# Two hybrid transformer blocks on one core: a written order of loads and smaller steps in the second block's attention stage

## The chip, the cores and the metric

The kernel runs on one core of a Trainium2 chip. The core has a matrix engine (TensorE, PE in the profile; its weight loads are PEld), a vector engine (VectorE, DVE), a scalar engine (ScalarE, ACT), GpSimd (POOL) and SyncE (SP). Each engine executes its own instructions in the order in which they stand in its stream, and waits on semaphores. DMAs are issued from SP, ACT or POOL and carried out by 16 DMA engines. The metric is the time of one execution in microseconds (us).

## The reference, cut to what matters

`x` has 512 tokens of 1024 channels, in float32. A first block (four mixers and a feed-forward network) is followed by a second one. The change touches only the first half of the second block:

```
h = rms(x, norm1) * (1 + sc1) + sh1
u, q, k, v = split(h @ w_in)             # 512 | 512 | 128 | 128 columns
# S5: a diagonal complex scan over the tokens, 32 groups of 16 channels, 64 states each
y = C_re s_re - C_im s_im + d_skip * u   # s = scan(a, B u)
z = gelu(y)
y_ssm = z * sigmoid(z @ w_glu + b_glu)
# attention: 8 query heads, 2 key/value heads, window of 128 tokens, one sink per head
q, k = rms(q per head), rms(k per head)
y_attn = softmax(q k / 8 + relative bias, with sink) v
x = x + g1 * (concat(rms(y_ssm), rms(y_attn)) @ w_out)
```

A modulated, gated feed-forward network with a convolution of width 3 follows and is unchanged.

## The kernel before

Activations lie transposed, channels on the 128 partitions and 512 tokens along the row. Every large product is done three times with numbers split into a high and a low part (`whi`, `wlo` for weights, `hl` for activations). A weight piece comes in with one SP DMA into a `raw` buffer (two of them), ACT copies its high part, and DVE subtracts the low part; for `w_glu` and `w_out` (w6, w7) ACT writes minus the high part and a POOL DMA adds the weights to it. There are five pairs of `whi`/`wlo`. A piece is loaded when the piece ahead of it is first used.

The stage of the second block is a list of steps, ORDER, of which PE's instructions are issued in exactly this order (`manual_schedule` with PE alone). What the other engines, SP included, do is ordered by a planner at build time: it takes an instruction when its data are ready by the planner's own estimate of times, and of those that are ready the one that stands earlier in the program. On the chip each engine then runs this fixed order, whatever the real times are.

The steps: `U` finishes the product for `u` and sends it through DRAM (`d_u`) to the layout of the scan (`ua`). `kp`, `qp` project keys and values, or queries, for two token tiles, copy the result out of PSUM (`tok`, and `v`) and norm it per head (`head_norm`: DVE, with two small ACT functions between); `kt`, `qt` transpose it. For each quarter q of the S5 channels, `a` is the product with `et`, copied to `z`; `b` rotates `z` by the tables `co`, `si` and runs eight scans on DVE; `c` rotates back into `sp`; `d` makes the outputs `ys` with the tables `tt`, `gt` and sends them through DRAM (`d_z`, eight small stores a quarter), reads them back as `yt` and adds the skip term. `e` is the gelu and the split for `g`, the gated unit. `s`, `t`, `v` are scores and softmax, transposes, and the product with the values, for one head group and token tile. `R`, `p`, `A` are the norms and the output product.

The copies out of PSUM run on ACT or DVE as a letter of EN says (`a`, `v`). The tables `et`, `co`, `si` of all four quarters and `tt`, `gt` of the first two are issued on SP before the list of steps; `tt`, `gt` of the others in step c2; the relative bias `relb` in the first score step of a head group. Buffers that matter: `tab` (six) for `et`, `tt`, `relb` and the probabilities, `tabg` (two) for `gt`, `sp` (two), PSUM `acc` (three), `sc` and `tr` (two each).

Of the kernel before, what the change touches and what calls it, by code (L numbers as in the profile page):

```python
# [17 lines left out]
P = 128  # L18
# [19 lines left out]
NPOS2 = 2  # L38
B2 = 1
TAIL = 4  # L40
ZQ = "assssaaa"
HP = ""
EG = 0
EN = "avaaavaaaaaaaaaaaaavvvvvvvavavvaaaavaaaaaaaaaaaavaavvvvavvvvaaaavvvvaavvvaaaaavavaaavaavvavvvvvvvvvvavvaavvvvvavvaaavaaaavaaavvaaaaaaavvvvvvvaaaaaaaaavvvavvaavaaaav"
EN_AT = {'k1': (0, 4), 'v1': (4, 4), 'q1': (8, 12), 'h1': (20, 8), 'w1': (28, 8), 's1': (36, 8), 'o1': (44, 16), 't1': (60, 46), 'u2': (106, 4), 'z2': (110, 4), 'y2': (114, 4), 'k2': (118, 2), 'v2': (120, 2), 'q2': (122, 4), 'h2': (126, 12), 's2': (138, 12), 't2': (150, 14)}
ORDER = "U kp0 kp1 a0 a1 kt0 b0 qp0 c0 a2 b1 qp1 kt1 b2 c1 d0 a3 c2 qt0 qt1 b3 c3 d1 s0 qp2 s1 s2 t0 d2 t1 d3 e0 s3 e1 qt2 t2 s4 qp3 v0 t3 s5 v1 g0 qt3 g1 g2 t4 g3 s6 v2 v3 s7 t5 R p0 p1 v4 p2 t6 v5 p3 p4 v6 t7 p5 v7 p6 p7 A"
NW = 16
NHL = 5
SUM_E = "vector"
# [183 lines left out]
def build(tc, I, out, PV, PVN, CS, CSN, CS1, CSN1):  # L233
# [1162 lines left out]
    def wt(nm):  # L1396
        return bp.tile([P, S], F32, tag="w", bufs=NW2, name=nm)

    def tab(nm):
        return bp.tile([P, 1024], F32, tag="tab", bufs=6, name=nm)  # L1400

    zT, zhl = [], []
    zs, z2s, cs, ss, sps, ets, tts, gts = {}, {}, {}, {}, {}, {}, {}, {}

    def s5_load(qs):
        for q in qs:
            ets[q] = tab("et")
            nc.sync.dma_start(ets[q], d_et[q])
            cs[q], ss[q] = wt("co"), wt("si")
            nc.sync.dma_start(cs[q], d_rot[q][:, 0])  # L1410
            nc.sync.dma_start(ss[q], d_rot[q][:, 1])

    def s5_load2(qs):
        for q in qs:
            tts[q] = tab("tt")
            nc.sync.dma_start(tts[q], d_t[q].rearrange("p g x -> p (g x)"))
            gts[q] = bp.tile([P, 8, 9 * 16], F32, tag="tabg", bufs=2, name="gt")
            nc.sync.dma_start(gts[q].rearrange("p g x -> p (g x)"), d_g[q])

    s5_load((0, 1))  # L1420
    s5_load2((0, 1))
    s5_load((2, 3))

    def u_out(q, ps):
        t = wt("uT").rearrange("p (s c) -> p s c", s=8)
# [52 lines left out]
            V.tensor_tensor_scan(z2[:, c], mag8[:, q * 8 + g:q * 8 + g + 1].to_broadcast([P, 64]), z[:, c], 0.0, ALU.mult, ALU.add)  # L1478

    def s5_c(q):  # L1480
        if q == 2:
            s5_load2((2, 3))
        z, z2 = zs[q], z2s[q]
        crossed(z, z2, ss[q], -1.0)
        zc = wt("zc")
        (G if "c" in ZC else V).tensor_tensor(zc, z2, cs[q], op=ALU.mult)
        sp = bp.tile([P, 8, 65], F32, tag="sp", bufs=2, name="sp")
        sps[q] = sp
        V.memset(sp[:, :, 0:1], 0.0)
        V.tensor_tensor(sp[:, :, 1:65], z.rearrange("p (g c) -> p g c", g=8),  # L1490
                        zc.rearrange("p (g c) -> p g c", g=8), op=ALU.add)

    def s5_d(q):
        ut = wt("ut")
# [9 lines left out]
            E.dma_start(d_z[q].rearrange("g h t c -> t h g c")[t], ys[16 * t:16 * t + 16])  # L1504
        yt = xp.tile([P, S], F32, tag="x", name="yt")
        nc.gpsimd.dma_start(yt, d_z[q].rearrange("g h t c -> (g h) (t c)"))
        V.scalar_tensor_tensor(yt, ut, V1("ssm_d", q), yt, op0=ALU.mult, op1=ALU.add)
        zT.append(yt)

    def s5_e(n):  # L1510
        if EG and n == 0:
            return
        for q in (range(4) if EG else (2 * n, 2 * n + 1)):
            ge = act(zT[q], zT[q], AF.Gelu_apprx_tanh)
            zz = hl()
            split(zz, zT[q])
            zhl.append(zz)
        tables(ge)
# [16 lines left out]
    def q_p(n):  # L1535
        j, m = n // 2, n % 2
        ps = acc()
        for u in range(2):
            proj_t(ps, wkv[1 + j], h, 2 * m + u, 256, 256 * u)
        qt, qn = wt("tok"), wt("tokn")  # L1540
        copy("q2", n, qt, ps)
        head_norm(bp, wt, [qn.rearrange("p (h a d) -> p h a d", h=8, a=1)], qt, 8)
        tokn["q", n] = qn.rearrange("p (u b x) -> p u b x", u=2, b=2)

# [13 lines left out]


    mixed = [hl() for _ in range(8)]  # L1560
    relbs, probs, pvs = {}, {}, {}
    tot_s, tot_a, r_s, r_a = (wt(n) for n in ("tot_s", "tot_a", "r_s", "r_a"))

    def keep(k, src, cs, tot, first, gain, n, scale=1.0):
# [14 lines left out]
    def swa_s(n):  # L1579

        kv, i, j0, W = window(n)
        if i == 0:
            relbs[kv] = tab("relb").rearrange("p (h y) -> p h y", h=4)
            nc.sync.dma_start(relbs[kv].rearrange("p h y -> p (h y)"), I["relb"][:, kv * 1024:(kv + 1) * 1024])
            V.tensor_scalar(relbs[kv], relbs[kv], -1.0, None, op0=ALU.mult)
        ml = bp.tile([P, 4], F32, tag="ml", bufs=2, name="ml")
        sl = bp.tile([P, 4], F32, tag="sl", bufs=2, name="sl")
        se = bp.tile([P, 4], F32, tag="se", bufs=2, name="se")
# [69 lines left out]
    def ssm_out(k):  # L1658
# [5 lines left out]
        V.scalar_tensor_tensor(t, ps, gm[:, k:k + 1], r_s, op0=ALU.mult, op1=ALU.mult)  # L1664
        G.tensor_tensor(x[k], x[k], t, op=ALU.add)

    steps = dict(U=u_last, a=s5_a, b=s5_b, c=s5_c, d=s5_d, e=s5_e, kp=kv_p, kt=kv_t, qp=q_p, qt=q_t,
                 s=swa_s, t=swa_t, v=swa_v, g=glu, R=norm_s, p=ssm_out, A=norm_a)
    with tc.manual_schedule(engines={mybir.EngineType.PE}):
        for step in ORDER.split():  # L1670
            name = step.rstrip("0123456789")
            with tc.high_priority() if name in HP.split(",") else nullcontext():
                steps[name](*([int(step[len(name):])] if step != name else []))
# [93 lines left out]
```

## Time and profile before

| what | value |
|---|---|
| median of 3 runs | 1274.1 us (1273.36 to 1276.45) |
| the profiled execution, its own time | 1273.53 us |
| its span in the trace | 1271.8 us |
| PE busy | 1220.6 us, 96% of the span |
| PEld busy | 986.8 us, 78% |
| DVE busy | 888.4 us, 70% |
| ACT busy | 512.6 us, 40% |
| POOL busy | 251.8 us, 20% |
| mean granted PE clock | 0.984 |

The page divides the span into 40 slices of about 32 us each and gives each engine's share in tenths. A "chain" is followed back from the last instruction. An arrow as in `PE <- DVE v` means that PE stood idle until the DVE instruction that writes `v` was done.

### The profile page before, as it was taken

How to read it: one execution, taken by the hardware profiler on the slowest of the kernel's cores; microseconds unless marked ns; L12 is line 12 of the kernel's file. 1: busy time of each engine (PE TensorE's matmuls, PEld its weight loads, DVE VectorE, ACT ScalarE, POOL GpSimd, SP SyncE). 2: the span in 40 equal slices, each digit the busy share in tenths (PEclk: the TensorE clock that was granted, in tenths of full speed). 3: DMA queues.
4: the chain of work that ended last, by engine and by line, in shares of the span. 5: the costliest groups of instructions: out<-in, count | busy, mean ns of one | idle time of the engine just before them, and what ended most of it. 6: DMA issues, size and time to landing. Idle time of an engine off the chain costs nothing.

```text
span 1271.8 us, 17124 instructions
## 1 busy us (share of the span) xinstructions
PE 1220.6 (96%) x6269; PEld 986.8 (78%) x6269; DVE 888.4 (70%) x1666; ACT 512.6 (40%) x874; POOL 251.8 (20%) x355
## 2 busy tenths in 40 slices
PE   7899999999999999999999978879999999999998
PEld 6788756567887888878889877758888888888887
DVE  7667858768877967777567578766887655555552
ACT  6334466453333332232324334764643423233330
POOL 1000003103408375573402232022000000000000
PEclk9999999999999999999999986989999999999999
DMA  6531111115466665656546873464364433323321
GB/s 222 150 124 51 51 33 50 51 42 167 131 182 180 214 211 191 200 171 211 171 149 235 241 190 96 111 169 101 92 186 120 123 93 99 99 83 99 100 83 66
DMA packets 165395, 169.87 MB, mean 134 GB/s; under 512 B 12352, under 2 KB 127952, under 8 KB 165312
## 3 DMA queue, kind: packets, MB, share of 16 engines
q1 hardware_dynamic: 154528, 146.96, 38.1%
q0 software_dynamic: 5696, 17.54, 5.4%
q10 hardware_dynamic: 5088, 4.29, 1.0%
q8 instruction: 49, 0.80, 0.3%
q14 instruction: 34, 0.28, 0.1%
HBM read 155.15 MB, written 15.43 MB: 134 GB/s over the span
## 4 chain that ended last, share of the span: by engine, by line
PE 81%; DVE 8%; issue 3%; ACT 3%; DMA 3%; POOL 1%; SPq 0%; POOLq 0%; ACTq 0%; DVEq 0%
PE acc L261 53%; PE sc L261 13%; PE tr L261 10%; PE po L261 2%; DMA raw<-in_w_dram 2%; DVE wlo L381 1%; PE tr L886 1%; ACT whi L374 1%; PE tr L1616 1%; DVE z L1478 1%; DVE z L1467 1%; DVE z L1466 1%; POOL keep L929 0%; DMA ua<-d_u 0%; DVE keep L930 0%
## 5 line engine op out<-in xcount | busy, mean ns | idle before, releaser
L261 PE MATMUL acc<-hl,whi 128*128 128x512 f32 (+1 forms) x1624 | 482.5, 380 | 9.5 <-ACT whi L374 6.1
L374 ACT ACTIVATE whi<-raw 128x1024 fp32r<-128x1024 f32 (+2 forms) x188 | 194.3, 1035 | 409.9 <-PE acc L261 230.6
L261 PEld LDWEIGHTS acc<-hl,whi 128*128 128x128 f32 x1624 | 294.4, 188 | 76.3 <-issue 8.8
L261 PE MATMUL acc<-hl,wlo 128*128 128x512 f32 (+1 forms) x812 | 307.6, 379 | 0.0
L381 DVE TENSOR_TENSOR wlo<-raw,whi 128x1024 fp32r<-128x1024 f32 (+2 forms) x178 | 226.1, 1272 | 110.2 <-ACT whi L374 106.0
L261 PEld LDWEIGHTS acc<-hl,wlo 128*128 128x128 f32 x812 | 152.7, 188 | 30.8 <-issue 2.4
L261 PE MATMUL acc<-hd,whi 128*128 128x512 f32 (+1 forms) x472 | 143.1, 386 | 2.1 <-DVE x L1348 2.1
L261 PE MATMUL acc<-whi,hl 128*128 128x256 f32 (+1 forms) x544 | 111.9, 297 | 6.6 <-DVE v L250 3.3
L261 PEld LDWEIGHTS acc<-hd,whi 128*128 128x128 f32 x472 | 86.9, 188 | 21.7 <-issue 3.1
L261 PEld LDWEIGHTS acc<-whi,hl 128*128 128x128 f32 x544 | 91.4, 200 | 12.0 <-DVE v L250 3.5
L261 PE MATMUL acc<-hd,wlo 128*128 128x512 f32 (+1 forms) x236 | 90.9, 385 | 0.0
L261 PE MATMUL acc<-wlo,hl 128*128 128x256 f32 (+1 forms) x272 | 80.2, 295 | 0.7 <-DVE wlo L381 0.7
L1082 DVE CUSTOM_DVE_ANT_0 wm<-wm,cb 128x512 f32<-128x512 f32 x96 | 75.5, 820 | 5.7 <-DMA wm<-in_wmod_dram 5.6
L261 PE MATMUL tr<-hl,whi 128*128 128x512 f32 (+1 forms) x240 | 72.8, 386 | 0.0
L261 PE MATMUL sc<-hl,whi 128*128 128x512 f32 x208 | 64.9, 393 | 0.0
L261 PEld LDWEIGHTS acc<-wlo,hl 128*128 128x128 f32 x272 | 54.6, 201 | 2.5 <-DVE wlo L381 1.0
L261 PEld LDWEIGHTS tr<-hl,whi 128*128 128x128 f32 x240 | 44.5, 188 | 9.8
L261 PEld LDWEIGHTS acc<-hd,wlo 128*128 128x128 f32 x236 | 44.3, 188 | 9.5
L929 POOL TENSOR_SCALAR_AFFINE_SELECT keep<-keep 128x128 f32<-128x128 f32 x16 | 9.3, 595 | 187.1 <-ACT keep L923 186.3
L261 PE MATMUL tr<-hl,wlo 128*128 128x512 f32 (+1 forms) x120 | 46.3, 386 | 0.0
L261 PEld LDWEIGHTS sc<-hl,whi 128*128 128x128 f32 x208 | 39.1, 188 | 9.0
L1348 DVE TENSOR_TENSOR x<-x,acc 128x512 f32<-128x512 f32 (+1 forms) x49 | 31.6, 655 | 19.2 <-PE acc L261 19.2
(427 smaller groups left out, 1893.5 us busy)
## 6 DMA issues: line engine op xcount, KB each, us to landing
raw<-in_w_dram SPq DMA_DIRECT2D x176, 512.0 KB, 4.3
wm<-in_wmod_dram SPq DMA_DIRECT2D x96, 256.0 KB, 4.0
wlo<-in_w_dram POOLq DMA_DIRECT2D x10, 512.0 KB, 7.9
xk<-in_xT_dram SPq DMA_DIRECT2D x16, 256.0 KB, 4.7
raw<-in_w_dram SPq DMA_DIRECT2D x10, 256.0 KB, 3.2
d_g<-s5g POOLq DMA_DIRECT2D x4, 576.0 KB, 4.6
gt<-d_g SPq DMA_DIRECT2D x4, 576.0 KB, 6.6
w1c<-in_w1k_dram SPq DMA_DIRECT2D x8, 256.0 KB, 5.8
```

The lines of the kernel that those rows point to most:

```text
L261: nc.tensor.matmul(o, lhsT=l, rhs=r, start=start, stop=stop, **k)
L374: act(v(hi)[:, a:b], v(raw)[:, a:b], AF.Copy)
L381: V.tensor_tensor(v(lo)[:, a:b], v(raw)[:, a:b], v(hi.bitcast(F32))[:, a:b], op=ALU.subtract)
L886: nc.tensor.transpose(tp[:, q * P:(q + 1) * P], pr[hh][:, j * P:(j + 1) * P], ident)
L929: G.affine_select(g[:, d], g[:, d], fill=1.0, **past)
L1082: V.tensor_tensor_reduce(wm, wm, cb[:, n * 512:(n + 1) * 512], 1.0, 0.0, ALU.mult, ALU.add, mh[:, n, j:j + 1])
L1348: done[0] = V.tensor_tensor(x[k][:, cs], x[k][:, cs], ps[:, cs], op=ALU.add)
L1466: V.scalar_tensor_tensor(dst[re], src[im], sign, t[im], op0=ALU.mult, op1=ALU.mult)
L1467: V.scalar_tensor_tensor(dst[im], src[re], -sign, t[re], op0=ALU.mult, op1=ALU.mult)
L1478: V.tensor_tensor_scan(z2[:, c], mag8[:, q * 8 + g:q * 8 + g + 1].to_broadcast([P, 64]), z[:, c], 0.0, ALU.mult, ALU.add)
L1616: nc.tensor.transpose(tp[:, m * P:(m + 1) * P], probs[n][:, hh, (j - j0) * P:(j - j0 + 1) * P], ident)
```

## The change

- Query norms become steps of their own (`qn`), and adding the skip term too (`y`, chained so that the quarters come in order). `kt1` stands ahead of `qp1`.
- The loads become steps: `L` (et, co, si of one quarter), `M` (tt, gt of one quarter), `B` (relb and its negation), and `W`, which loads the next weight piece. The loads of SP are issued in the order of the list, as PE's are.
- All four gelus run in `e1`, the last quarter first, the others queued behind it on ACT; `e0` is gone.
- Four copies go from DVE to ACT: `z` of quarters 1 and 2, `ys` of quarter 2, `v` of the second pair of token tiles (in EN: z2 `avva` to `aaaa`, y2 `aava` to `aaaa`, v2 `av` to `aa`).
- Of the eight `d_z` stores of a quarter four were on SP and four on ACT; now four are on POOL and four on ACT.

```diff
--- before.py
+++ after.py
@@ -38,12 +38,12 @@
 NPOS2 = 2
 B2 = 1
 TAIL = 4
-ZQ = "assssaaa"
+ZQ = "aggggaaa"
 HP = ""
 EG = 0
-EN = "avaaavaaaaaaaaaaaaavvvvvvvavavvaaaavaaaaaaaaaaaavaavvvvavvvvaaaavvvvaavvvaaaaavavaaavaavvavvvvvvvvvvavvaavvvvvavvaaavaaaavaaavvaaaaaaavvvvvvvaaaaaaaaavvvavvaavaaaav"
+EN = "avaaavaaaaaaaaaaaaavvvvvvvavavvaaaavaaaaaaaaaaaavaavvvvavvvvaaaavvvvaavvvaaaaavavaaavaavvavvvvvvvvvvavvaavvvvvaaaaaaaaaaaaaaavvaaaaaaavvvvvvvaaaaaaaaavvvavvaavaaaav"
 EN_AT = {'k1': (0, 4), 'v1': (4, 4), 'q1': (8, 12), 'h1': (20, 8), 'w1': (28, 8), 's1': (36, 8), 'o1': (44, 16), 't1': (60, 46), 'u2': (106, 4), 'z2': (110, 4), 'y2': (114, 4), 'k2': (118, 2), 'v2': (120, 2), 'q2': (122, 4), 'h2': (126, 12), 's2': (138, 12), 't2': (150, 14)}
-ORDER = "U kp0 kp1 a0 a1 kt0 b0 qp0 c0 a2 b1 qp1 kt1 b2 c1 d0 a3 c2 qt0 qt1 b3 c3 d1 s0 qp2 s1 s2 t0 d2 t1 d3 e0 s3 e1 qt2 t2 s4 qp3 v0 t3 s5 v1 g0 qt3 g1 g2 t4 g3 s6 v2 v3 s7 t5 R p0 p1 v4 p2 t6 v5 p3 p4 v6 t7 p5 v7 p6 p7 A"
+ORDER = "U L0 kp0 L1 kp1 M0 a0 a1 kt0 b0 qp0 L2 b1 M1 c0 a2 W qn0 c1 kt1 W qp1 L3 d0 B0 b2 a3 W M2 c2 qn1 b3 c3 qt0 qt1 d1 M3 y0 s0 qp2 s1 s2 t0 y1 d2 t1 d3 s3 qn2 y2 y3 e1 qt2 t2 B1 s4 qp3 qn3 v0 t3 s5 v1 g0 qt3 g1 g2 t4 g3 s6 v2 v3 s7 t5 R p0 p1 v4 p2 t6 v5 p3 p4 v6 t7 p5 v7 p6 p7 A"
 NW = 16
 NHL = 5
 SUM_E = "vector"
@@ -1399,27 +1399,30 @@
     def tab(nm):
         return bp.tile([P, 1024], F32, tag="tab", bufs=6, name=nm)
 
-    zT, zhl = [], []
+    zT, zhl, relbs = [], [], {}
     zs, z2s, cs, ss, sps, ets, tts, gts = {}, {}, {}, {}, {}, {}, {}, {}
 
-    def s5_load(qs):
-        for q in qs:
-            ets[q] = tab("et")
-            nc.sync.dma_start(ets[q], d_et[q])
-            cs[q], ss[q] = wt("co"), wt("si")
-            nc.sync.dma_start(cs[q], d_rot[q][:, 0])
-            nc.sync.dma_start(ss[q], d_rot[q][:, 1])
-
-    def s5_load2(qs):
-        for q in qs:
-            tts[q] = tab("tt")
-            nc.sync.dma_start(tts[q], d_t[q].rearrange("p g x -> p (g x)"))
-            gts[q] = bp.tile([P, 8, 9 * 16], F32, tag="tabg", bufs=2, name="gt")
-            nc.sync.dma_start(gts[q].rearrange("p g x -> p (g x)"), d_g[q])
-
-    s5_load((0, 1))
-    s5_load2((0, 1))
-    s5_load((2, 3))
+    def s5_load(q):
+        ets[q] = tab("et")
+        nc.sync.dma_start(ets[q], d_et[q])
+        cs[q], ss[q] = wt("co"), wt("si")
+        nc.sync.dma_start(cs[q], d_rot[q][:, 0])
+        nc.sync.dma_start(ss[q], d_rot[q][:, 1])
+
+    def s5_load2(q):
+        tts[q] = tab("tt")
+        nc.sync.dma_start(tts[q], d_t[q].rearrange("p g x -> p (g x)"))
+        gts[q] = bp.tile([P, 8, 9 * 16], F32, tag="tabg", bufs=2, name="gt")
+        nc.sync.dma_start(gts[q].rearrange("p g x -> p (g x)"), d_g[q])
+
+    def ahead():
+
+        next(p_ for p_ in queue if p_.parts is None).load()
+
+    def relb_load(kv):
+        relbs[kv] = tab("relb").rearrange("p (h y) -> p h y", h=4)
+        nc.sync.dma_start(relbs[kv].rearrange("p h y -> p (h y)"), I["relb"][:, kv * 1024:(kv + 1) * 1024])
+        V.tensor_scalar(relbs[kv], relbs[kv], -1.0, None, op0=ALU.mult)
 
     def u_out(q, ps):
         t = wt("uT").rearrange("p (s c) -> p s c", s=8)
@@ -1478,8 +1481,6 @@
             V.tensor_tensor_scan(z2[:, c], mag8[:, q * 8 + g:q * 8 + g + 1].to_broadcast([P, 64]), z[:, c], 0.0, ALU.mult, ALU.add)
 
     def s5_c(q):
-        if q == 2:
-            s5_load2((2, 3))
         z, z2 = zs[q], z2s[q]
         crossed(z, z2, ss[q], -1.0)
         zc = wt("zc")
@@ -1489,6 +1490,8 @@
         V.memset(sp[:, :, 0:1], 0.0)
         V.tensor_tensor(sp[:, :, 1:65], z.rearrange("p (g c) -> p g c", g=8),
                         zc.rearrange("p (g c) -> p g c", g=8), op=ALU.add)
+
+    uts, ys_ = {}, []
 
     def s5_d(q):
         ut = wt("ut")
@@ -1504,14 +1507,20 @@
             E.dma_start(d_z[q].rearrange("g h t c -> t h g c")[t], ys[16 * t:16 * t + 16])
         yt = xp.tile([P, S], F32, tag="x", name="yt")
         nc.gpsimd.dma_start(yt, d_z[q].rearrange("g h t c -> (g h) (t c)"))
-        V.scalar_tensor_tensor(yt, ut, V1("ssm_d", q), yt, op0=ALU.mult, op1=ALU.add)
         zT.append(yt)
+        uts[q] = ut
+
+    def s5_y(q):
+        with tc.issue_after(ys_[0].ins) if ys_ else nullcontext():
+            ys_[:] = [V.scalar_tensor_tensor(zT[q], uts[q], V1("ssm_d", q), zT[q], op0=ALU.mult, op1=ALU.add)]
 
     def s5_e(n):
-        if EG and n == 0:
-            return
-        for q in (range(4) if EG else (2 * n, 2 * n + 1)):
-            ge = act(zT[q], zT[q], AF.Gelu_apprx_tanh)
+
+        ge = act(zT[3], zT[3], AF.Gelu_apprx_tanh)
+        for q in range(3):
+            with tc.issue_after(ge.ins):
+                ge = act(zT[q], zT[q], AF.Gelu_apprx_tanh)
+        for q in range(4):
             zz = hl()
             split(zz, zT[q])
             zhl.append(zz)
@@ -1537,8 +1546,11 @@
         ps = acc()
         for u in range(2):
             proj_t(ps, wkv[1 + j], h, 2 * m + u, 256, 256 * u)
-        qt, qn = wt("tok"), wt("tokn")
-        copy("q2", n, qt, ps)
+        tokn["q", n] = wt("tok")
+        copy("q2", n, tokn["q", n], ps)
+
+    def q_n(n):
+        qt, qn = tokn["q", n], wt("tokn")
         head_norm(bp, wt, [qn.rearrange("p (h a d) -> p h a d", h=8, a=1)], qt, 8)
         tokn["q", n] = qn.rearrange("p (u b x) -> p u b x", u=2, b=2)
 
@@ -1558,7 +1570,7 @@
 
 
     mixed = [hl() for _ in range(8)]
-    relbs, probs, pvs = {}, {}, {}
+    probs, pvs = {}, {}
     tot_s, tot_a, r_s, r_a = (wt(n) for n in ("tot_s", "tot_a", "r_s", "r_a"))
 
     def keep(k, src, cs, tot, first, gain, n, scale=1.0):
@@ -1579,10 +1591,6 @@
     def swa_s(n):
 
         kv, i, j0, W = window(n)
-        if i == 0:
-            relbs[kv] = tab("relb").rearrange("p (h y) -> p h y", h=4)
-            nc.sync.dma_start(relbs[kv].rearrange("p h y -> p (h y)"), I["relb"][:, kv * 1024:(kv + 1) * 1024])
-            V.tensor_scalar(relbs[kv], relbs[kv], -1.0, None, op0=ALU.mult)
         ml = bp.tile([P, 4], F32, tag="ml", bufs=2, name="ml")
         sl = bp.tile([P, 4], F32, tag="sl", bufs=2, name="sl")
         se = bp.tile([P, 4], F32, tag="se", bufs=2, name="se")
@@ -1664,9 +1672,9 @@
         V.scalar_tensor_tensor(t, ps, gm[:, k:k + 1], r_s, op0=ALU.mult, op1=ALU.mult)
         G.tensor_tensor(x[k], x[k], t, op=ALU.add)
 
-    steps = dict(U=u_last, a=s5_a, b=s5_b, c=s5_c, d=s5_d, e=s5_e, kp=kv_p, kt=kv_t, qp=q_p, qt=q_t,
+    steps = dict(L=s5_load, M=s5_load2, B=relb_load, W=ahead, qn=q_n, y=s5_y, U=u_last, a=s5_a, b=s5_b, c=s5_c, d=s5_d, e=s5_e, kp=kv_p, kt=kv_t, qp=q_p, qt=q_t,
                  s=swa_s, t=swa_t, v=swa_v, g=glu, R=norm_s, p=ssm_out, A=norm_a)
-    with tc.manual_schedule(engines={mybir.EngineType.PE}):
+    with tc.manual_schedule(engines={mybir.EngineType.PE, mybir.EngineType.SP}):
         for step in ORDER.split():
             name = step.rstrip("0123456789")
             with tc.high_priority() if name in HP.split(",") else nullcontext():
```

## Rows read from the trace of the kernel before

**Rows 1.** The page: TensorE's granted clock in 40 slices of the span.

```profile
PEclk9999999999999999999999986989999999999999
```

**Rows 2.** PE's waits in 705 to 890 us: total us, times, longest.

```profile
PE sc L261 <- DVE ml L1598: 6.5, 2, 5.6
PE tr L1549 <- DVE tokn L540: 6.5, 1, 6.5
PE acc L261 <- DVE v L250: 3.3, 1, 3.3
PE acc L261 <- DMA raw<-in_w_dram: 1.8, 1, 1.8
PE tr L1616 <- DVE q2T L251: 1.8, 1, 1.8
...
PE tr L1616 <- DVE prob L1608: 1.3, 1, 1.3
```

**Rows 3.** Windows of single steps: us, PE, PEld, DVE, ACT, POOL busy, PEclk, DMA share, GB/s.

```profile
736.00:744.40 8.40, 8.40 (x49) 8.40 (x50) 6.01 (x11) 1.90 (x5) 2.19 (x2) 0.65 0.88 227
775.10:783.00 7.90, 7.90 (x52) 7.68 (x50) 7.73 (x23) 0.00 (x0) 1.80 (x2) 0.73 0.57 158
804.90:810.80 5.90, 5.90 (x50) 5.76 (x48) 4.03 (x16) 3.94 (x9) 0.55 (x1) 1.00 0.51 190
...
758.80:765.40 6.60, 0.06 (x2) 0.04 (x1) 5.77 (x14) 1.48 (x4) 2.25 (x2) 0.77 0.90 281
```

**Rows 4.** A window of 10 us, same columns.

```profile
760.00:770.00 10.00, 3.97 (x18) 3.81 (x19) 9.09 (x22) 3.06 (x8) 2.16 (x3) 0.62 0.62 184
```

**Rows 5.** ACT's timeline: start us, us, ..., [idle before <- releaser].

```profile
731.07 1.06 ACT L374 ACTIVATE whi<-raw 128x1024 fp32r<-128x1024 f32 x1 [1.95 <-DMA raw<-in_w_dram]
734.16 1.06 ACT L377 ACTIVATE wlo<-raw 128x1024 fp32r<-128x1024 f32 x1 [2.04 <-DMA raw<-in_w_dram]
735.12 0.37 ACT L248 ACTIVATE tok<-acc 128x256 f32<-128x256 f32 x1
```

**Rows 6.** SP's timeline: weight loads, and a load of x.

```profile
706.59 30.20 SPq L356 DMA_DIRECT2D raw<-in_w_dram  x8
...
825.94 0.38 SPq L356 DMA_DIRECT2D raw<-in_w_dram  x1
828.21 0.32 SPq L1662 DMA_DIRECT2D x<-d_x  x1
```

**Rows 7.** DMA engines in 706 to 730 us.

```profile
DMA packets 2462, 6.35 MB, mean 265 GB/s; under 512 B 403, under 2 KB 403, under 8 KB 2460
```

**Rows 8.** DMA issues in 685 to 860 us: count, size, median us to landing.

```profile
gt<-d_g SPq DMA_DIRECT2D x4, 576.0 KB, 6.6
...
yt<-d_z POOLq DMA_DIRECT2D x4, 256.0 KB, 3.0
...
d_z<-ys SPq DMA_DIRECT2D x16, 32.0 KB, 2.2
```

**Rows 9.** DVE's timeline.

```profile
739.62 0.68 DVE L250 COPY z<-acc 128x512 f32<-128x512 f32 x1
...
774.17 0.07 DVE L1489 MEMSET sp<- 128x8 f32 x1 [2.19 <-PE acc L261]
...
810.08 0.75 DVE L1507 SCALAR_TENSOR_TENSOR yt<-ut,pv,yt 128x512 f32<-128x512 f32 x1 [1.66 <-DMA yt<-d_z]
```

**Rows 10.** POOL's timeline: two DMA issues.

```profile
785.31 1.08 POOL L1495 DMA_DIRECT2D ut<-d_u  x2
```

**Rows 11.** ACT's timeline: tables, gelu, and a weight split.

```profile
788.80 1.28 ACT L1514 ACT_TABLE_LOAD   x1
...
810.86 0.63 ACT L1514 ACTIVATE yt<-yt 128x512 f32<-128x512 f32 x1 [1.99 <-DVE yt L1507]
...
834.58 1.06 ACT L374 ACTIVATE whi<-raw 128x1024 fp32r<-128x1024 f32 x1 [4.12 <-DMA raw<-in_w_dram]
```

**Rows 12.** PE's timeline: the first product of the gated unit.

```profile
814.49 0.73 PE L261 MATMUL acc<-hl,whi 128*128 128x512 f32 x2
```

## The prediction

> **What bounds the kernel now.** I read the page first, then PE's waits, then the windows, then the timelines. PE's granted clock dips near the start, in the last slice, and around three fifths of the way [rows 1]. That last place, about 705 to 890 us, is the stretch that the change touches. Everything outside it stays, so the whole gain or loss has to be found there.
>
> In this stretch PE's matmuls are the work that must be done, and the waits are what can be won. The longest [rows 2]: 6.5 us before a transpose that needs the normed queries (`tokn`), 5.6 us for `ml` (attention scores), 3.3 us for the copy `v`, 1.8 us put down to a weight DMA. A second cost follows a long wait: PE comes back at the lower of its two levels, 1.2 instead of 2.4 GHz. One query projection takes 8.4 us after the 3.3 us wait, at a mean granted clock of 0.65; a later one takes 5.9 us at 1.00 [rows 3]: 2.5 us more.
>
> The 6.5 us wait is not idleness of the kernel. In 758.8 to 765.4 DVE works 5.77 of 6.60 us [rows 3], in 760 to 770 it works 9.09 of 10 while PE has 3.97 [rows 4]. DVE has the scan steps and both norms in one line and is the bound there. The 3.3 us wait comes from ACT's order instead: two splits of prefetched weights wait for their DMAs, 1.95 and 2.04 us, and the copy of `tok`, for which a PSUM buffer is held, runs behind them only at 735.12 [rows 5].
>
> **The change, part by part.** The sum is made against the profiled execution, 1273.5 us, 0.6 below the median shown, 1274.1; its span is 1271.8.
>
> *Loads in a written order, weights ahead.* Today the rotation and table loads (L, M) are issued ahead of the weights; SP's eight weight loads start at 706.59 and spread over 30 us, each waiting for one of two raw buffers [rows 6]. After the change L1, M0, L2 and M1 stand between the same weight loads. By the shapes in the code an L is 512 + 256 + 256 KB, and an M is 512 and 576 [rows 8], so the four groups have 4.2 MB. In 706 to 730 the engines moved 265 GB/s [rows 7]: 16 us for the four. About 2.6 MB of L and M (10 us) stand ahead of the first weight now and are gone from there. The early weights come sooner, the last two of the series later, by 16 - 10 = 6 us if nothing else gives. Bounds: the wait of 3.3 and the slow projection's 2.5 vanish (-5.8), or both weight waits of ACT grow by the 6 us (+6). Both ends are equally near; I take 0. The 1.8 us wait has as much traffic ahead of it as now; I take -1, ends -1.8 and 0. The W steps load the same pieces as now, hidden under PE's projections: 0; without that cover a split costs ACT its 1.06 us [rows 5]. `relb` is loaded and negated earlier by the same two instructions: 0.
>
> *Copies on the scalar engine.* Four copies leave DVE: two `z` and one `ys` of 128x512 at 0.68 [rows 9], and a `v` of half the width, estimated at 0.4: 2.4 us. Three lie in or before the stretch where DVE is the bound. They cost ACT about the same; it has 3.06 of 10 us there [rows 4]. If ACT is stuck again they wait behind it (the slower rival). I take -2.4, ends -2.4 and 0.
>
> *Query norms as steps of their own.* The instructions are the same; they move behind the scan steps c0 and c2 in the planner's order. DVE's sum up to the attention scores is unchanged: PE gets the second queries later, by b2 and c2, but the scores and what follows them no later. What can go is a wait of DVE's own, 2.19 us: at 774.17 a MEMSET of a scan buffer stands in DVE's line until PE is done with the buffer [rows 9], and the next scan sum, whose data are there, waits behind it. With PE's work in another phase I take -2.1; ends -8.5 (the 6.5, and the 2.0 by which the projection from 775.1 is slower than 5.9 us [rows 3]) and +3 (the MEMSET waits on, and PE's longer wait is no longer covered). kt1 ahead of qp1 is four transposes of keys normed long before: 0.
>
> *d_z on other queues.* Sixteen small stores go from SP to POOL. POOL issues two DMAs in 1.08 us [rows 10], so a tile's four take 2.2 us, and their landing may be like POOL's 3.0 instead of SP's 2.2 [rows 8]: +0.8 for the data that y3 waits for. POOL's products for the scans stand in the same line, but POOL is busy only 2.16 of 10 us there [rows 4].
>
> *One gelu chain.* Six table loads around the gelus (three in, three back) become two: four of 1.28 us [rows 11], 5.1 us less on ACT. But all gelus now come behind the last one. y3 starts at 810.08 and takes 0.75 [rows 9]; a load 1.28, four gelus and a split at 0.63 [rows 11], the low part 0.68: 810.08 + 5.86 = 815.9 for the gated unit's first operand. PE starts that unit at 814.49 [rows 12]: +1.4, with d_z +2.2. ACT's relief reaches the scores and probabilities ahead of it, with waits of 1.8 and 1.3 us [rows 2]; I credit 3 of these 3.1. Gelu and d_z together -0.8, ends -3.1 and +2.2.
>
> *The 5.6 us wait.* ACT stands 4.12 us for a weight at 834.58 [rows 11], and the scaled copy that DVE, and after it PE, need stands behind it. With SP in program order that weight's load goes behind a load of x that waits for the gated unit's output: 828.21 instead of 825.94 [rows 6]. Then the planner knows that it is late and can put the copy first. Ends: -8 (5.6, and as much for the slow clock behind it as in the projection, 2.5) and +2.3 (the later issue, and ACT's order as now). I take -2.7.
>
> Sum: 0 - 1 - 2.4 - 2.1 - 0.8 - 2.7 = -9.0, so 1264.5 us.
>
> One rule speaks against the d_z part. The rows show POOL's DMA issues at 0.54 us each, and no wait inside one [rows 10]. The Trainium skill, "DMA: Bandwidth & Descriptors", section "SWDGE vs HWDGE vs iDMA", says that POOL writes descriptors into on-chip state from which DVE, in some of its modes, locks it out, and that SP's and ACT's queues are immune. The trace has no instance of it so far; what it would do is among the rivals.
>
> **The rivals.** *Slower: ACT stuck behind late weights.* Place: 731 to 743 us. ACT executes in order, and the planner has put splits ahead of copies once already [rows 5]. Price: the two weight waits grow by the 6 us above; `tok` is copied at 741 instead of 735, and the projection, the `z` copies (now all on ACT) and the scans follow 6 us later. 6 - 2.4 for the copies + 2.2 for gelu and d_z = +5.8: 1279 us. It decides from where the last two weights come some 3 us later than now. For it: the DMA engines already run at 265 GB/s. Against: the first weights come sooner, and a new plan may order ACT otherwise. Chance 0.22.
>
> *No change: DVE keeps the pace.* The long waits go on in other places, because DVE's sum falls by 2.4 us only and gelu and d_z take 2.2 back; with the 1 us of the weight wait 1272.3 us. For it: DVE's 5.77 of 6.60 us. Against: PE's clock losses come on top of DVE's pace. Chance 0.18.
>
> *More: the waits go whole.* ACT is not stuck (-5.8), the query norm's wait goes by 5, the copies give 2.4, the 5.6 us wait goes with its clock (-8), gelu and d_z cost 2.2: -19, 1254.5 us. For it: none of these waits is work. Against: all would have to go at once. Chance 0.17.
>
> *d_z on POOL bites.* Each of a tile's four stores waits for one DVE instruction of 0.68: 2.7 us more per tile, and the scans' products behind them too. If two tiles reach PE: +5.4, 1270 us, still faster than before. That is the lockout of the skill's page as a mechanism of this kernel. For it: DVE at 9 of 10. Against: the 0.54 us issues. Chance 0.08.
>
> **How the numbers follow.** The likeliest has 0.35: 1264.5, own range 1259 to 1269. A change of 0.3% is 3.8 us, about what a measurement of this kernel can tell from none. Faster: 0.35 + 0.17 + 0.08 = 0.60; same 0.18, slower 0.22. The range takes in the case of more and most of the slower one, 1252 to 1279; about 0.06 is left below and 0.12 above.
>
> **What would show it.** Right: the second `tok` copy of the key projections near 727 to 735 and not 741; the `tokn` wait shorter or moved, with DVE still near 9 of 10; no MEMSET that waits for PE; two table loads at the gelus, and a PE wait of 1 to 3 us ahead of the gated unit; no 4 us wait of ACT for a weight between that unit's outputs. Wrong: DMA engines full from 710 to 740 with PE's wait there doubled (slower), or PE's clock at its upper level all through the stretch, which is worth more than I give it.

## The result, and the profile after

The changed kernel takes 1292.1 us (median of four runs, 1287.2 to 1292.8) against 1273.7 us of the kernel before on the same chip: a ratio of 1.0134, 95% interval 1.0107 to 1.0161. It is slower by 17 us, where 1264.5 us was forecast and 1279 was the top of the range. The profiled execution is the fastest of the four: 1287.2 us, span 1285.5. So its trace, read against the one before (span 1271.8), accounts for 13.7 of the 17 us.

TensorE's waits in 705 to 890 us, as in [rows 2] (total us, times, longest), and the clock of the page, as in [rows 1]:

```profile
PE tr L1561 <- DVE tokn L540: 31.9, 3, 19.6
PE sc L261 <- DVE ml L1606: 5.2, 2, 4.3
PE tr L1624 <- DVE q2T L251: 2.4, 1, 2.4
...
PE acc L261 <- ACT whi L374: 0.9, 1, 0.9
PE acc L261 <- DVE wlo L381: 0.9, 1, 0.9
```

```profile
PEclk9999999999999999999999977789999999999999
```

Of the waits of [rows 2], `v` (3.3) and the weight DMA (1.8) are gone; two of 0.9 us for the halves of a weight, the last two lines of the first view, stand in place of the second. The one for the normed queries went from 6.5 us in one piece to 31.9 in three, two of them long. Windows, columns as in [rows 3]: 736 to 744.4, where one projection ran at a clock of 0.65, is at 1.00 throughout. But then PE has nothing at all for 10 us, and DVE, which did 9.09 of 10 us there before [rows 4], does 3.20:

```profile
736.00:744.40 8.40, 8.40 (x75) 8.40 (x74) 8.14 (x15) 1.98 (x5) 3.63 (x3) 1.00 1.02 365
...
760.00:770.00 10.00, 0.00 (x0) 0.00 (x0) 3.20 (x9) 0.00 (x0) 3.25 (x4) 0.50 0.63 169
770.00:780.00 10.00, 5.99 (x29) 6.02 (x29) 9.67 (x20) 2.07 (x6) 2.98 (x3) 0.50 0.26 48
...
804.30:815.80 11.50, 0.01 (x1) 0.00 (x1) 7.01 (x21) 6.22 (x15) 4.11 (x7) 0.61 0.70 218
```

**The first long wait (19.6 us, in front of qt1).** DVE's timeline, then POOL's, then SP's:

```profile
762.22 0.69 DVE L527 TENSOR_TENSOR nsq<-tok 128x512 f32<-128x512 f32 x1
769.63 1.74 DVE L1491 TENSOR_TENSOR sp<-z,zc 128x512 f32<-128x512 f32 x1 [6.72 <-POOL zc L1487]
771.29 0.67 DVE L529 TENSOR_REDUCE nss<-nsq 128x8 f32<-128x512 f32 x1
...
773.17 0.69 DVE L540 TENSOR_TENSOR tokn<-tok,nr 128x512 f32<-128x512 f32 x1
```

```profile
754.56 2.58 POOL L1507 DMA_DIRECT2D d_z<-ys  x4
757.16 1.28 POOL L1477 TENSOR_TENSOR zc<-z,co 128x512 f32<-128x512 f32 x1
766.75 0.60 POOL L1509 DMA_DIRECT2D yt<-d_z  x1 [8.31 <-DMA d_z<-ys]
...
767.96 1.64 POOL L1487 TENSOR_TENSOR zc<-z,co 128x512 f32<-128x512 f32 x1
```

```profile
752.57 0.33 SPq L356 DMA_DIRECT2D raw<-in_w_dram  x1
753.14 0.33 SPq L1414 DMA_DIRECT2D tt<-d_t  x1
753.57 0.37 SPq L1416 DMA_DIRECT2D gt<-d_g  x1
754.26 0.33 SPq L1414 DMA_DIRECT2D tt<-d_t  x1
```

Read it from PE backwards. The norm of the second queries (`nsq` to `tokn`) is cut in two by c2's sum, which stands in its line and waits 6.7 us for POOL's product. POOL's product stands behind the read-back of `yt`, which waits 8.3 us until the stores of `d_z` have landed. And the stores land late: SP, in its written order, sends a weight and three tables (2.1 MB) in the same 2 us, and POOL's own loads of `wlo` and `ut` (0.8 MB, issued at 753.4 and 754.0) come on top. In 754.5 to 766 the DMA engines moved 264 GB/s at a share of 0.88, so 2.9 MB take about 11 us, an estimate from these numbers. The landings in 752 to 768 us (median us in the last column; before, the median of all four quarters was 2.2 [rows 8], and one quarter's stores, beside one 576 KB load, took 3.3 to 6.2):

```profile
d_z<-ys ACTq DMA_DIRECT2D x4, 32.0 KB, 10.6
d_z<-ys POOLq DMA_DIRECT2D x4, 32.0 KB, 9.8
```

Both queues are late alike, so POOL's issuing is not the reason: its four issues took 2.58 us, near the 2.2 that the prediction took from [rows 10].

**The second (11.5 us, in front of qt2).** `yt` of quarter 2 now stands behind the first store of quarter 3 on POOL, and that store behind ScalarE's copy; on DVE the add y2 waits 4.05 us for it in the middle of query norm 2:

```profile
807.22 0.54 POOL L1507 DMA_DIRECT2D d_z<-ys  x1 [4.75 <-ACT ys L248]
808.34 0.57 POOL L1509 DMA_DIRECT2D yt<-d_z  x1 [0.59 <-DMA d_z<-ys]
```

```profile
812.18 0.75 DVE L1515 SCALAR_TENSOR_TENSOR yt<-ut,pv,yt 128x512 f32<-128x512 f32 x1 [4.05 <-DMA d_z<-ys]
...
814.99 0.69 DVE L540 TENSOR_TENSOR tokn<-tok,nr 128x512 f32<-128x512 f32 x1
```

The same milestones in both kernels and six of the variants below (starts in us from the span's start: the first use of c0's sum in d0, the transposes of qt1, qt2 and qt3, the first score maxima `ml` on DVE, PE's product that takes the sum `tot_a` at the stretch's end; last column: the idle time of DVE from 740 us to the first maxima, its length less DVE's busy time there):

| profile | d0 | qt1 | ml | qt2 | qt3 | tot_a | DVE idle |
|---|---|---|---|---|---|---|---|
| before | 753.1 | 765.4 | 776.3 | 800.8 | 819.2 | 872.8 | 6.0 |
| after | 747.6 | 774.0 | 783.0 | 815.8 | 835.5 | 886.5 | 11.8 |
| qn12_early | 751.7 | 763.1 | 786.4 | 808.9 | 832.6 | 884.0 | 10.5 |
| b_qn | 753.5 | 774.5 | 783.5 | 815.8 | 832.5 | 882.0 | 3.9 |
| b_loads | 750.2 | 759.6 | 783.5 | 810.6 | 831.2 | 883.7 | 11.4 |
| best1 | 748.2 | 759.4 | 776.1 | 797.5 | 822.8 | 873.8 | 2.2 |
| best2 | 750.9 | 760.8 | 778.4 | 801.2 | 826.5 | 877.2 | 3.3 |
| best3 | 752.7 | 763.3 | 781.8 | 807.9 | 833.0 | 884.5 | 7.0 |

The change brings PE to d0 5.4 us sooner, is 6.7 us behind at the first maxima, and loses 7.0 more by `tot_a`. DVE's added idle time of 5.8 us is near the first loss in size, but it does not decide by itself: b_qn reaches the maxima as late (783.5) with only 3.9 us idle.

### The profile page after: what moved, and what is told of

Read it like the earlier page. It is cut to its first block, busy times and chain, and to the rows that moved or that the text cites. A ratio compares the mean times of both kernels' runs of the same rounds, so it can differ in the third digit from the quotient of the medians.

```text
span 1285.5 us, 17126 instructions
## 1 busy us (share of the span) xinstructions
PE 1216.7 (95%) x6269; PEld 983.3 (76%) x6269; DVE 887.8 (69%) x1662; ACT 508.9 (40%) x874; POOL 262.7 (20%) x371
## 4 chain that ended last, share of the span: by engine, by line
PE 80%; DVE 7%; DMA 5%; issue 4%; ACT 3%; POOL 1%; ACTq 0%; SPq 0%; POOLq 0%; DVEq 0%
PE acc L261 53%; PE sc L261 13%; PE tr L261 9%; PE po L261 2%; DMA raw<-in_w_dram 2%; DMA d_z<-ys 1%; PE tr L886 1%; DVE wlo L381 1%; ACT whi L374 1%; DMA d_u<-uT 1%; POOL keep L929 0%; DVE z L1469 0%; DMA wlo<-in_w_dram 0%; DVE keep L930 0%; PE tr L941 0%
```

## The experiments

Each was timed beside the kernel before (medians 1272.2 to 1273.3 in the four groups); ratios are to it, with 95% intervals.

**First group: is it the norm's place, POOL's line, the burst, or the queue?**

`qn_early`
```diff
-... d0 B0 b2 a3 W M2 c2 qn1 b3 ...
+... d0 qn1 B0 b2 a3 W M2 c2 b3 ...
```


> The changed kernel with one step of the written order moved: query norm 1 stands right behind step d0, ahead of steps b2 and c2, not behind c2. Theory A (the norm is held by what stands ahead of it in VectorE's line): its token copy ends at 753.5 in the changed kernel, and the norm costs 0.7 + 0.7 + 0.5 (ScalarE) + 0.5 + 0.7 us, so the transposes of qt1 start near 758 instead of 774.0 and their wait falls from 19.6 to about 4 us; the second wait (11.5 us, in front of qt2) stays; the whole comes to about 1275 us (ratio to the kernel before 1.000 to 1.004). Theory B (the stores of d_z on GpSimd's queue hold GpSimd, and with it the scans, wherever the norm stands): the wait moves to the next reader of c2's sum, step d2, and the whole stays above 1284 us.

Measured: 1.0146 (1.0123 to 1.0168), no gain. qt1 came at 760.9, as theory A had it, but PE then waits 5.5 us for the first maxima (the other of the two waits in the second line, 4.3 us, is in the changed kernel too). Ahead of these maxima DVE has the sums of c2 and c3, and b2 before them, held 6.7 us for a product of POOL's behind the read-back. So theory B was right about the time; the wait in front of qt2 stayed (11.3 us):

```profile
PE tr L1561 <- DVE tokn L540: 11.3, 1, 11.3
PE sc L261 <- DVE ml L1606: 9.8, 2, 5.5
```

`read_back`
```diff
     def s5_c(q):
-        (G if "c" in ZC else V).tensor_tensor(zc, z2, cs[q], op=ALU.mult)
+        zci = (G if "c" in ZC else V).tensor_tensor(zc, z2, cs[q], op=ALU.mult)
+        if q == 2:
+            with tc.issue_after(zci.ins):
+                read_back(0)      # the load of yt, taken out of s5_d(0)
```


> The changed kernel with the read-back of quarter 0 (the load of yt from d_z on GpSimd's queue) issued behind step c2's product instead of ahead of it, and step y0's add behind query norm 1 on VectorE; the loads and the stores are as in the changed kernel. Theory A1 (GpSimd's in-order line: the read-back waits 8.3 us for the landing of the stores, and c2's product behind it): c2's product runs near 763 instead of 768, the wait in front of qt1 falls from 19.6 to 11 to 13 us, the whole by 6 to 8 us, to about 1280 us. Theory A2 (only the place of the norm behind c2): the wait in front of qt1 stays near 19 us and the whole within 2 us of the changed kernel, 1287 to 1292 us.

Measured: 1.0097 (1.0076 to 1.0118), 5 us less than the changed kernel. The wait fell to 8.9 us, but the new plan also brought d0 6.4 us later and put y0's add behind query norm 1, and qt1 started at 773.5 against 774.0: the run doesn't tell A1 from A2, and where the 5 us come from is not seen in its one profile, which is of the slowest of its four executions.

`tt_early`
```diff
-... c0 a2 W qn0 ...
+... c0 a2 W T2 T3 qn0 ...     # T loads tt; M2 and M3 load only gt
```


> The changed kernel with the tables tt of quarters 2 and 3 loaded some 15 us sooner, ahead of the second load of weights in the written order of the sync engine, so that they no longer go out in the same 2 us as quarter 0's stores of d_z. Theory A1 with the burst as its origin: the eight stores land in 2 to 4 us instead of 10, the wait in front of qt1 falls from 19.6 to 9 to 13 us, the whole to 1279 to 1283 us. If the burst is not the origin, the stores still land in 8 us or more and the time stays at 1287 us or above.

Measured: 1.0080 (1.0061 to 1.0099), 7 us less than the changed kernel. qt1's wait was 11.4 us, as expected, but the stores still took 7.6 and 8.0 us: the tables were not the whole burst. In this plan c2's product also stood ahead of the read-back; the run doesn't tell to which of the two the 7 us are due.

`z_act`
```diff
-ZQ = "aggggaaa"
+ZQ = "aaaaaaaa"
```


> The changed kernel with all eight stores of d_z of each quarter on ScalarE's queue, none on GpSimd's. Theory A1: in this order c2's product stands ahead of the read-back of quarter 0, and the read-back of quarter 2 no longer stands behind the first store of quarter 3 on GpSimd, so the first wait falls by 6 to 8 us and the second by 3 to 6 us; the four more issues cost ScalarE 2.2 us a quarter; the whole comes to about 1277 us. Theory B (GpSimd's stores are the whole cause): both waits go nearly whole, 1265 to 1270 us. Theory C (neither queue matters, only the norm's place): no change, 1286 us or above.

Measured: 1.0137 (1.0120 to 1.0155), no gain: A1's and B's numbers fail, and C's is met for another reason. c2's product did run ahead of the read-back, but the eight stores held ScalarE. Its timeline, first with the eight in one row, then the same in two windows:

```profile
759.32 11.36 ACTq L1507 DMA_DIRECT2D d_z<-ys  x8
770.78 0.60 ACT L248 ACTIVATE z<-acc 128x512 f32<-128x512 f32 x1 [11.49 <-DMA d_z<-ys]
...
773.16 0.29 ACT L512 ACTIVATE nr<-nss,eps 128x8 f32<-128x8 f32 x1
```

```profile
759.32 1.90 ACTq L1507 DMA_DIRECT2D d_z<-ys  x4
...
768.85 1.82 ACTq L1507 DMA_DIRECT2D d_z<-ys  x4
```

The 11.36 us are not issuing. Four stores went out in 1.90 us and the other four in 1.82; between them ScalarE stood 7.6 us. The fifth store counts on the same semaphore as the first and waits for it, and the first landed at 768.83. So the late landing held ScalarE by a wait of the program's own, and the root of query norm 1, whose sum was ready at 770.1, came behind a copy and two weight halves at 773.16.

**Second group: the norms, and the first parts alone.**

`qn2_early`, `qn12_early`
```diff
-... s0 qp2 s1 ... s3 qn2 y2 ...
+... s0 qp2 qn2 s1 ... s3 y2 ...        # qn12_early: and qn1 behind d0
```


> The changed kernel with query norm 2 alone moved: right behind the projection qp2 (its place in the kernel before), not behind step s3. In the changed kernel the transposes of qt2 start at 815.8 after a wait of 11.5 us, and start between 812.5 and 820.8 in each of the four variants, whatever those did in front of qt1. Theory D (the place behind s3 pins this: VectorE takes the norm up only after s3's maxima, and ScalarE computes its root behind s3's exponentials): the wait goes to under 1.5 us, qt2 starts near 805, the whole falls by 8 to 12 us to 1276 to 1282 us. Theory E (the late landing of quarter 2's stores and of yt, in front of which VectorE stands, pins it): the adds y2 and y3 then hold VectorE in front of step s4 instead, the wait moves to the score products, and the whole stays above 1284 us.

> The changed kernel with query norm 1 right behind step d0 and query norm 2 right behind qp2. If the places of the two norms carry the loss (theories A and D), both waits go: the move of norm 1 alone brought qt1 13 us forward and lost it again by qt2, with the second one gone at least a part of it stays, 1264 to 1274 us. If GpSimd's hold of the scans (the read-back of quarter 0 ahead of b2's product) is what binds once norm 1 is out of the way, the time is that of moving norm 2 alone, within 3 us.

Measured: 1.0101 (1.0084 to 1.0118) and 1.0091 (1.0066 to 1.0116). With norm 2 at its old place the wait in front of qt2 is gone (theory D), and 4 us of the time with it, not 8 to 12, and at the edge of what the intervals tell; norm 1 on top gives nothing that can be told. With both away POOL's hold is bare: the read-back stands ahead of b2's product, and DVE waits for that. POOL's and DVE's timelines of qn12_early:

```profile
770.53 0.59 POOL L1509 DMA_DIRECT2D yt<-d_z  x1 [9.06 <-DMA d_z<-ys]
771.13 1.29 POOL L1477 TENSOR_TENSOR zc<-z,co 128x512 f32<-128x512 f32 x1
```

```profile
772.45 0.69 DVE L1478 TENSOR_TENSOR z<-zc,z 128x512 f32<-128x512 f32 x1 [8.12 <-POOL zc L1477]
```

`b_qn`
The kernel before, with the norm of a query projection in a step of its own:
```diff
-... b1 qp1 ... c2 qt0 ... e0 s3 e1 ... qp3 v0 ...
+... b1 qn0 qp1 ... c2 qn1 qt0 ... e0 s3 qn2 e1 ... qp3 qn3 v0 ...
```


> The kernel before with the query norms alone split off and put at the changed kernel's places (0 behind b1, 1 behind c2, 2 behind s3, 3 behind qp3); copies, loads, gelu and stores as before. If the places of the norms carry the loss by themselves, this is 10 us or more slower than the kernel before: 1283 to 1292 us, with a wait of about 10 us in front of qt2. If it takes the loads or the stores of the changed kernel to make them late, within 4 us of the kernel before.

Measured: 1.0055 (1.0032 to 1.0077), 7 us, between its two cases. So the places of the norms cost by themselves, with no wait of DVE for POOL ahead of qt1: the waits for `tokn` are 25.6 us in three, 10.9 in front of qt1 and 11.0 in front of qt2 among them. (Quarter 0's stores took 3.4 to 9.5 us to land here too, all issued on SP and ScalarE as before.)

`b_copies`
The kernel before:
```diff
-EN = "...vvvavvaaavaaaavaaavv..."
+EN = "...vvvaaaaaaaaaaaaaaavv..."
```


> The kernel before with the copies of PSUM in the steps a, d and qp on ScalarE alone, as in the changed kernel. The prediction has -2.4 us for it, from 0.7 us of VectorE on the path at each of three stalls: 1271 us. If ScalarE's in-order line (weights' halves and the norms' roots ahead of the copies) costs more than that, 1274 us or above.

Four copies move, two of `z`, one `ys` and one `v`, and none of qp, though the expectation names it. Measured: 1.0004 (0.9989 to 1.0019). Nothing, in a band of -1.4 to +2.4 us.

**Third group: the other parts alone, and a mended version.**

`b_zpool`
The kernel before:
```diff
-ZQ = "assssaaa"
+ZQ = "aggggaaa"
```


> The kernel before with the four middle stores of d_z of each quarter on GpSimd's queue instead of the sync engine's, alone. In its order the read-back of quarter 0 stands behind c2's and b3's products on GpSimd, so the hold of the changed kernel can't come up there; the read-back of quarter 2 stands behind the first store of quarter 3. If the queue by itself is what costs: 1280 us or above. If it costs only in company with the burst of loads: 1272 to 1276 us. The prediction had +0.8 us.

Measured: 1.0058 (1.0036 to 1.0080): +7.4 us; the median, 1280.2, just meets the first case's bound of 1280. Quarter 0's stores landed in about 2 us here, and no store took over 3.3, so lateness isn't the reason. POOL's order does change: the read-back of quarter 2 stands behind quarter 3's first store (806.4, against 799.6 before), and that of quarter 3 comes at 814.9, against 805.0. But that it is the cause is not shown. In this execution (1285.6 us, the slowest of six) PE is level with the kernel before at the first maxima (775.5 against 776.3) and already 5.8 us behind at qt2 (806.6 against 800.8), with no wait over 1.7 us on the way but a lower clock in 793 to 806.6, 0.50 against 0.87. The two late read-backs lie at the end of that stretch or behind it, where 4.9 us more are lost by `tot_a`:

```profile
805.61 0.54 POOL L1504 DMA_DIRECT2D d_z<-ys  x1 [5.21 <-ACT ys L248]
806.41 0.57 POOL L1506 DMA_DIRECT2D yt<-d_z  x1 [0.26 <-issue]
807.96 1.82 POOL L1504 DMA_DIRECT2D d_z<-ys  x3 [0.97 <-issue]
814.87 0.59 POOL L1506 DMA_DIRECT2D yt<-d_z  x1 [5.10 <-issue]
```

`b_gelu`
The kernel before, with e1 as in the changed kernel:
```diff
-... d3 e0 s3 ...
+... d3 s3 ...
...
+        ge = act(zT[3], zT[3], AF.Gelu_apprx_tanh)
+        for q in range(3):
+            with tc.issue_after(ge.ins):
+                ge = act(zT[q], zT[q], AF.Gelu_apprx_tanh)
```


> The kernel before with the four gelus as one chain behind the last of the adds, two table loads instead of six, alone. The prediction has 5.1 us less on ScalarE, of which 3 us are credited, and 1.4 us more for the gated unit: -1.6 us, 1272 us. If the late first gelu costs what the theory of the changed kernel's late adds says, a wait of PE in front of the gated unit's first product and 1276 us or above.

Measured: 1.0002 (0.9981 to 1.0023). Nothing that can be told, in a band of -2.4 to +2.9 us.

`b_loads`
The changed kernel with the copies and gelus of before, norms and adds next to their projections and steps d; left are SP's written order, the stores on POOL, kt1 ahead of qp1 and the order of the adds:
```diff
-... qp0 L2 b1 M1 c0 a2 W qn0 c1 kt1 W qp1 L3 d0 B0 ... c2 qn1 b3 ... d1 M3 y0 s0 qp2 s1 s2 t0 y1 d2 t1 d3 s3 qn2 y2 y3 e1 ...
+... qp0 qn0 L2 b1 M1 c0 a2 W c1 kt1 W qp1 qn1 L3 d0 y0 B0 ... c2 b3 ... d1 y1 M3 s0 qp2 qn2 s1 s2 t0 d2 y2 t1 d3 y3 e0 s3 e1 ...
```


> The changed kernel with everything taken back but two parts: the loads in a written order with the weights ahead, and the stores of d_z on GpSimd's queue (which the kernel before with these stores alone is to be compared with). Copies, query norms, adds and gelus are as in the kernel before. If the burst of tables and weights against the stores is the other half of the loss (the query norms alone gave +7 us), this has stores landing in 8 us or more, the scans held by GpSimd, and 1279 us or above; if the loads' order is free, as the prediction took it, 1273 to 1276 us.

Measured: 1.0096 (1.0073 to 1.0119), 4.8 us on top of b_zpool (by the two intervals, anything from about 1 to 9). The stores landed in 9.4 and 10.5 us and POOL waited 7.7, as expected. In DVE's line the wait of the MEMSET for PE, 2.19 us before [rows 9], had grown to 5.9:

```profile
767.45 0.07 DVE L1490 MEMSET sp<- 128x8 f32 x1 [5.89 <-PE acc L261]
```

`best1`: the changed kernel with the edits of qn12_early, tt_early and read_back together.

> The changed kernel with four things put right at once: query norm 1 behind d0, query norm 2 behind qp2, the tables tt of quarters 2 and 3 ahead of the second load of weights, and the read-back of quarter 0 behind c2's product on GpSimd. If these are the whole cause, the clock losses of the long waits go too, and the time falls below the kernel before, 1262 to 1271 us. If the late adds y2 and y3 and the one gelu chain cost as well (with both norms out of the way VectorE still stood 2.8 us for y2, and PE 2 us each for what stands behind it), 1273 to 1279 us. Above 1281 us something else binds.

Measured: 1.0048 (1.0025 to 1.0072), 11 us less than the changed kernel, 6 us more than the kernel before, as its second case had it. The profile is of the fastest of ten executions (1274.4, median 1277.4): in it the first maxima are where they were before, and PE is 1.0 us behind at `tot_a`.

**Fourth group: what is left.**

`z_sp` (the changed kernel), `no_qn_z` (with the edit of qn12_early), `best2` (best1)
```diff
-ZQ = "aggggaaa"
+ZQ = "assssaaa"
```


> The changed kernel with the four middle stores of d_z of each quarter back on the sync engine's queue, in its written order. If GpSimd's queue costs 7 us as it does on top of the kernel before, 1282 to 1285 us. If it was the late landing only, whichever queue, the time stays at 1287 us or above.

> The changed kernel with the stores back on the sync engine and query norms 1 and 2 early: what is left of the change is the written order of loads, the copies and the one gelu chain. If the loads cost by themselves, 1276 to 1281 us; if they cost only by delaying stores that GpSimd then waits for, within 3 us of the kernel before, 1270 to 1276 us.

> The mended version (norms early, tables tt early, read-back of quarter 0 behind c2's product) with the stores on the sync engine. In the mended version the last two read-backs ran at 799.6 and 806.4 behind quarter 3's stores on GpSimd, and PE lost 7 us against the kernel before between s3 and qt3. If that queue is the cause, 1268 to 1272 us; if the gelu chain behind the last add is, no gain, 1276 to 1279 us.

Measured: z_sp 1.0076 (1.0048 to 1.0105), no_qn_z 1.0071 (1.0049 to 1.0093), best2 1.0061 (1.0040 to 1.0082). Off POOL the stores cost the changed kernel 7 us less, as alone, which was z_sp's first case. Everything but the norms 1 and 2 and POOL's stores (loads, copies, adds, gelu chain, norms 0 and 3) still costs 9 us in no_qn_z. One reason is seen: with SP in program order the load of `relb` goes behind the stores, and DVE stands for it. Its timeline in no_qn_z:

```profile
766.96 0.69 DVE L1425 TENSOR_SCALAR relb<-relb 128x1024 f32<-128x1024 f32 x1 [1.92 <-DMA relb<-in_relb_dram]
```

For the mended version the sync engine is no better (1.0061 against 1.0048, intervals that overlap). That is the case of no gain, at 1280.9 us; its reason, the gelu chain, is not shown, and alone the chain costs nothing that can be told (b_gelu).

`best3`
best2 with a3 moved:
```diff
-... qp1 L3 d0 qn1 B0 b2 a3 W ...
+... qp1 L3 a3 d0 qn1 B0 b2 W ...
```


> As best2, with step a3 (16 products, 2 us of PE) ahead of step d0, whose second product waits 1.5 us for c0's sum in the mended version. If that wait is what puts TensorE on its lower clock for the 23 us behind it, the wait and the fall go, and PE saves up to 9 us there, of which 3 to 6 us should reach the end: 1262 to 1268 us. If VectorE's pace binds there anyway, the same as best2 within 2 us.

Measured: 1.0099 (1.0071 to 1.0128), 4.8 us worse than best2. The question came from best1: there PE waits 1.5 us at d0 and then runs 750 to 770 us at 0.50 though it is busy 18.6 of those 20. But best3 is best2 with a3 moved, and best2 has no wait at d0 and is at 1.00 in 750 to 760 already, so the run can't answer it. What it shows is that a3 costs at the new place: PE waits 1.7 us there for `et`, and 6.0 instead of 4.1 for `tokn`; on DVE the root that norm 1 needs and `relb` are late by 3.3 and 2.5 us (0.6 and 1.7 in best2), and the maxima come at 781.8 instead of 778.4. Windows of best1, best2 and best3:

```profile
750.00:760.00 10.00, 8.57 (x41) 8.20 (x41) 8.47 (x19) 6.91 (x13) 4.78 (x8) 0.50 0.67 173
760.00:770.00 10.00, 10.00 (x51) 9.66 (x50) 9.76 (x15) 1.51 (x4) 5.03 (x5) 0.50 0.71 172
```

```profile
750.00:760.00 10.00, 6.67 (x60) 6.43 (x59) 9.06 (x16) 4.37 (x9) 3.48 (x4) 1.00 0.44 85
760.00:770.00 10.00, 9.22 (x45) 8.90 (x46) 8.09 (x16) 3.94 (x7) 3.21 (x3) 0.50 0.64 193
```

```profile
750.00:760.00 10.00, 6.20 (x52) 5.85 (x52) 8.22 (x14) 3.86 (x7) 4.24 (x4) 1.00 0.21 38
760.00:770.00 10.00, 6.74 (x32) 6.77 (x33) 5.39 (x16) 1.25 (x3) 0.00 (x0) 0.56 0.84 241
```

## Why the prediction was wrong, point by point

*Query norms* (-2.1 forecast, ends -8.5 and +3; +7 measured alone): this is the step that failed. It said that PE gets the second queries later, "but the scores and what follows them no later". That left out PE's own work between the two: d1's products stand behind qt1 and take 7.7 us at the lower clock, and the scores come behind them. With the norm ahead of b2 and c2, PE did qt1 and d1 while DVE did b2 and c2; with the norm behind c2 the two are in series. In b_qn qt1 comes 9.1 us later and the maxima 7.2. Norm 2 behind s3 does the same in front of qt2 (it goes with qn2_early). The MEMSET that was to stop waiting still waits 1.8 us.

*d_z on other queues* (+0.8 forecast; +7.4 alone): the term was too small by 6.6 us. The issue time was right (2.1 to 3.0 us for a quarter's four, over all runs) and, where little else was under way, the landing (about 2). What was not seen is the order: POOL's read-back waits for a landing, and what POOL has behind it, products in the changed kernel and stores in b_zpool, waits with it. The changed kernel's trace shows what that costs (8.3 us on POOL, 6.7 on DVE); for b_zpool's 7.4 us it is not shown. The prediction looked for a hold of the scans' products in the rival *d_z on POOL bites*, but at the issue (each store waiting for a DVE instruction) and with a gain on balance. With these issue times no run here shows a hold of the size that the rival priced, 2.7 us more a tile. The Trainium skill, "DMA: Bandwidth & Descriptors", section "SWDGE vs HWDGE vs iDMA", states the lockout that the rival took up, DVE, in some of its modes, keeping POOL from the state into which it writes descriptors.

*Loads and ACT's order* (0, ends -5.8 and +6; +4.8 on top of b_zpool): what the prediction priced came out on its good side. The copy of `tok` runs at 728.9, `v`'s wait is gone, the projection keeps its clock, PE is 5.4 us ahead at d0. So the slower rival named the right side and the wrong place: ACT was not stuck behind weights. The cost came 10 us later, where the prediction set 0 for the W steps and for `relb`: tables written behind a weight that waits for its buffer go out with it, into the stores. The 1.8 us weight wait (-1) gave nothing: two of 0.9 stand in its place.

*Copies* (-2.4) and *gelu* (-1.6 without d_z): no effect was seen alone. The copies' -2.4 is outside the measured band (-1.4 to +2.4), the gelu's -1.6 inside it (-2.4 to +2.9), so that one isn't refuted. The table loads did go from six to two, and the first gelu waits 5.4 us for the last add.

*The 5.6 us wait* (-2.7, ends -8 and +2.3) is 4.3 us now: 1.3 less. ACT's 4.12 us for a weight is gone, as foreseen, but DVE is busy 9.03 of 9.20 us in 843 to 852.2, with the gated unit's outputs ahead of those maxima.

The rival *No change: DVE keeps the pace* comes nearest to what the traces show, though no run tests it by itself: PE came to d0 5.4 us sooner and to the first maxima 6.7 us later, since each wait put into DVE's line came on top of DVE's own work. The parts alone make 0.5 + 0.3 + 7.4 + 7.0 + 4.8 = 20 us against the 17 measured, each known to 2 to 4 us; they need not add up. The norms, which cost 7 alone, show nothing once the stores are off POOL: z_sp is only 0.05% above no_qn_z, well inside their intervals.

Open: what b_zpool's 7.4 us are due to, and why its PE ran at the lower clock in 793 to 806.6; what keeps best1 6 us above the kernel before; and what the clock behind the wait at d0 costs, which best3 could not test. No version beat the kernel before.

## What to carry to other kernels

Before a step is moved behind another on a busy engine, list what the engine that waits for it has to do between it and the next meeting point: work that ran beside the other engine now runs after it. Avoid leaving an instruction that waits for a DMA's landing ahead of products in the line of an engine that feeds the bound; ask of each read-back what stands behind it. Where the profile gives many DMA issues as one long row, look at them singly: part of the row can be a wait of the program's own, as in z_act. A load order written by hand needs the moment at which each blocked load is let go: what is queued behind it goes out in one burst, on whatever is small and urgent then.

## What was not expected of the hardware

Eight stores of 32 KB took 8.9 to 10.8 us to land beside 2.9 MB of loads (DMA share 0.88, 264 GB/s), on both queues alike, against 1.8 to 2.3 us for the first quarter before. And a wait of 1.5 us was followed by 20 us at the lower clock with PE busy 18.6 of them (best1), while after 1.8 us at the same product PE kept the full clock until its next wait, 1.8 us again (tt_early).
